# A hybrid streaming encoder on one core: diagonal blocks of the recurrent heads moved to GpSimd, one weight split moved in the pump, another lead-in

## The chip, the cores and the metric

The kernel runs on one core of a Trainium2 chip. The metric is the device time of one execution in microseconds; the number compared is the median of several runs. Engines in the profile: PE is TensorE's matmuls and PEld its weight loads, DVE is VectorE, ACT is ScalarE, POOL is GpSimd, SP is SyncE, which only issues transfers.

## The reference

One step of a one-layer encoder. A prompt of 512 new frames (no history) and a sample of 32 frames (with running state) go through the same layer: a normalisation, one wide input projection, then two branches side by side, merged by sigmoid gates, an output projection and a gated embedding. The first branch is an mLSTM with 4 heads, the second an HGRN2 with 8 recurrent heads of width 128. The change touches the second branch (and the first microseconds of the program). For one head and one chunk the reference does:

```python
g = jnp.cumsum(lf, axis=2)
dec = jnp.exp(jnp.where(causal, g[:, :, :, None, :] - g[:, :, None, :, :], -jnp.inf))
a = jnp.einsum('bhtc,bhtsc,bhsc->bhts', q, dec, k)
o = jnp.einsum('bhtc,bhce->bhte', q * jnp.exp(g), S) + jnp.einsum('bhts,bhse->bhte', a, v)
S_new = jnp.exp(g_last[:, :, 0, :])[..., None] * S + jnp.einsum('bhsc,bhse->bhce', k * jnp.exp(g_last - g), v)
```

So each query frame sees each earlier key frame through a decay of its own for every channel; a frame sees itself without decay, which is the diagonal of `a`. After that the output `o` of a head is normalised over its 128 channels and gated.

## The kernel before

**Data.** Activations lie with channels on partitions and 544 frames (32 of the sample, then 512 of the prompt) along the free axis. Each fp32 operand of a large matmul is split into a rounded high part and a low rest (`split_piece`: ScalarE casts the high part, VectorE subtracts), and a product is three matmuls: high x high, high x low, low x high, each 272 columns wide.

**Weights and the pump.** The wide projections run in pairs of output units (class `Two`) by a seven-product scheme for 2 x 2 blocks: the blocks are called a11, a12, s1, s2, s3, a22, s4, and the weight tiles carry these names and the unit's number (ws275 is s2 of unit 75). Each block is 12 matmuls in two halves of 6. The `Pump` holds all blocks of a stage in one order. One step of it is half a block: `pump.done` counts steps, and before block number i begins, `prepare(i + 1 + AHEAD)` issues the raw loads and the splits of blocks up to three ahead. `pump.behind` and `pump.pairs`, when they are set, bind a split's instructions behind another instruction of the same engine.

**Recurrent heads.** `heads()` is a generator that runs the attention of the 8 heads between the pump's steps: whatever it yields is the number of half blocks that TensorE does before it comes back, with the list `GAPS` giving most of them. TensorE's order is thus written by hand; VectorE, ScalarE and GpSimd are put in order by the compiler's scheduler, by the order of the program text and by readiness. In the profile the head's instructions lie from 628 to 876 us, with the blocks of the projections of the next heads between them, about 29.3 us a head.

Decays are applied by doubling distances: for each of 7 levels (distance 1, 2, 4, ... 64) `copies` saves the keys and queries that the level needs, `scores` makes the level's score blocks on TensorE, and `scale` multiplies keys and queries by the decay up to the next level (VectorE, L1936). Scores are made three times a head: for level 0 with the diagonal blocks (`diagonal`: 20 small matmuls), for the levels up to 8, and for the levels up to 64. Level 0 of the next head is made together with the last scores of this one. `collect` puts the scores of the levels together (VectorE's predicated copies at L1956, ScalarE's copies at L1958 and L1962). `masked` then spreads the near blocks with four GpSimd copies (L1977) and takes four triangles of 128 x 128 with GpSimd (`triangle`, L1792) into the tile `aa`.

After the last `scale(6)`, two steps later, `columns` transposes the scaled keys on TensorE (ht, L1819), `state` makes the new state (su), and some steps later `output` multiplies `aa` with the values (ho, L2012), adds the part from the state, and evacuates PSUM. The squares of the output's rows are summed on ScalarE (L2022), VectorE makes the inverse roots (L182 to L187) and scales the output (L2026), and `finish` transposes it back (hoT, L2103) and gates it (L2107).

The diagonal itself takes a path of its own in the kernel before: `collect` multiplies the diagonal blocks with a mask that keeps only their diagonals (`same`), sums each row to one number a frame (`dg`, L1953), `shares` multiplies the values with it on ScalarE (L1834, L1835) into the output tile `ov`, and `output` adds the matmuls' result on VectorE (L2018, L2019).

**Lead-in.** The first loads all go through SyncE's queue: input piece 0, first weight piece 0, input piece 1, and so on. TensorE runs 8 matmuls on a cleared tile before its first product.

Of the kernel before, what the change touches and what calls it, by code (L numbers as in the profile page):

```python
# [37 lines left out]
SUB = 5  # L38
LASTS = (0, 3, 6)
GAPS = (2, 2, 1, 3, 6, 2, 4, 2, 2, 4, 2, 8)  # L40
SLOT = 550
# [28 lines left out]
def hybrid_step(ctx: ExitStack, tc: tile.TileContext, a, o):  # L70
# [29 lines left out]
    def half(b):  # L100
        return slice(b * TH, (b + 1) * TH)
# [19 lines left out]

    def raw_piece(src, name):
        raw = wp.tile([P, WP], F32, tag="wr", name=name, bufs=NRAW)
        nc.sync.dma_start(raw[:, : src.shape[-1]], src)
        return raw
# [77 lines left out]
    def load(k):  # L203
        t = eslot(f"x{k}")
        nc.sync.dma_start(t[:, : T + 1], a["xT"][k])
        xt.append(t)
        wf.append([raw_piece(a["w_first"][k], f"wf{k}r")])

# [495 lines left out]
    class Pump:  # L704


        def __init__(self, todo):
            self.done, self.when, self.behind, self.pairs, self.limit, self.todo = 0, {}, None, None, None, todo
            order, base = [], 0
            for n, e in enumerate(todo):  # L710
# [682 lines left out]
    with tc.manual_schedule(engines={mybir.EngineType.Activation, mybir.EngineType.DVE, mybir.EngineType.PE}):  # L1393

        warm = small("warm", [P, P], bufs=1, tag="vsm")
        V.memset(warm, 0.0)
        wps = paux("warm")
# [7 lines left out]
        def products(k):  # L1405
            for f in range(NF):
                steps(acc[f], wf[k][1:], (k,), f * P, 0)

        for k in range(KD):
            t = xt[k]  # L1410
            hi, lo = pair_tile(f"x0{k}", k // (KD // 2))
            g = t[:, T : T + 1]
            S.mul(hi, t[:, :T], g)
            V.scalar_tensor_tensor(lo, t[:, :T], g, hi.bitcast(F32), ALU.mult, ALU.subtract)
            x0.append((hi, lo))
            wf[k].append(split_piece(wf[k][0], f"wf{k}", NF * P))
            if k == 1:
                load(KD - 2)
                load(KD - 1)
            sqk = slot(f"r0q{k}")[:, :T]  # L1420
            S.activation(sqk, t[:, :T], AF.Square)
            sq.append(sqk)
            if k in (1, 3):
                V.tensor_tensor(sq[k - 1], sq[k - 1], sqk, ALU.add)
            if k in (5, 6):
                i, j = ((0, 2), (4, 5))[k - 5]
                V.tensor_tensor(sq[i], sq[i], sq[j], ALU.add)
            if k > 1:
                products(k - 2)
# [368 lines left out]
    class Head:  # L1798


        def __init__(self, h):
# [7 lines left out]
            self.more = tp.tile([P, NA + 4 * NS], F32, tag="ksm", name=f"kx{h}", bufs=1)  # L1809
            self.dg, self.osb = small("dg", [P, 5]), small("osb", [P, P])  # L1810
            self.told, self.base, self.tsmp = self.tf[:, :T], 0, None
# [13 lines left out]
        def values(self):  # L1825
# [4 lines left out]
            nc.sync.dma_start(self.s0, a["S0"][self.h])  # L1830

        def shares(self):
            for b in range(NB):
                S.mul(self.ov[:, b * P : (b + 1) * P], self.it[:, b * P : (b + 1) * P], self.dg[:, b : b + 1])  # L1834
            S.mul(self.osb, self.its, self.dg[:, 4:5])  # L1835

# [86 lines left out]
        def scale(self, li):  # L1923
# [6 lines left out]
            for t, lo, m, first, _ in sides:  # L1930
# [4 lines left out]
                )  # L1935
                V.tensor_tensor(x, x, d, ALU.mult)  # L1936
            if told.shape[-1] == 2 * (nb + na):
# [6 lines left out]
            if c == NS // 2:  # L1944
                self.tsmp = tn[:, nb - 1 : nb]
            self.told = tn

        def collect(self):
            at = self.at
            if self.found[0][1] == 0:  # L1950
                same = self.kq[:, : (NB + 1) * NS].rearrange("p (b t) -> p b t", t=NS)
                V.tensor_tensor(same, self.pdg.rearrange("p (b t) -> p b t", t=NS), eye, ALU.mult)
                V.tensor_reduce(self.dg, same, AX.X, ALU.add)  # L1953
            for ps, li, c in self.found:
# [12 lines left out]
        def masked(self):  # L1967
# [39 lines left out]
        def output(self):  # L2007
# [9 lines left out]
            with tc.high_priority():  # L2017
                V.tensor_tensor(ov[:, :NP], po[:, 0, :], ov[:, :NP], ALU.add)  # L2018
                V.tensor_tensor(osb, po[:, 1, :P], osb, ALU.add)  # L2019
            hv, hr = small("hv", [P, 5]), small("hr", [P, 5])  # L2020
# [14 lines left out]
    def heads():  # L2035
# [9 lines left out]
        for h in range(HH):  # L2045
# [10 lines left out]
            x.copies(3)  # L2056
            x.shares()
            yield GAPS[3]
# [25 lines left out]
            x.collect()  # L2084
# [334 lines left out]
```

## Time and profile before

| | us |
|---|---|
| median of three runs | 1090.64 (1089.84 to 1091.63) |
| profiled execution, its own time | 1091.98 |
| its span in the trace | 1090.0 |
| TensorE matmuls busy | 1080.7 |
| VectorE busy | 897.3 |
| ScalarE busy | 700.3 |
| GpSimd busy | 217.2 |

The ends of matmuls are modelled, so a busy TensorE in this table still hides waits of a few tenths of a microsecond; they show in the starts of the matmuls. A timeline row has the start and the length in us, engine, line, operation, output and inputs, shapes and count; in brackets stands the idle time before it and what ended it. A row of a group has busy us and mean ns of one, then idle time of the engine before it.

### The profile page before, as it was taken

The page shows a single profiled execution, that of the slowest core. Times are in us where ns is not written, and L with a number is a line of the kernel's source. Part 1 is how long each engine was busy: PE and PEld are TensorE (multiplying, and loading weights), DVE is VectorE, ACT ScalarE, POOL GpSimd, SP SyncE. Part 2 cuts the span into 40 slices and gives each one's busy share as a digit, 9 for nine tenths or more (in the row PEclk, how much of TensorE's full clock was granted, in tenths as well). Part 3 has the DMA queues.
Part 4 walks back from the last instruction along what each step waited for, and adds up shares of the span by engine and source line. Part 5 has one row for each costly group of instructions (what it writes and reads, how often), then busy time and mean ns, then how long its engine had stood idle before and what let it go on. Part 6 is the DMA issues. An engine that isn't in the chain of part 4 may idle for free.

```text
span 1090.0 us, 26205 instructions
## 1 busy us (share of the span) xinstructions
PE 1080.7 (99%) x9865; PEld 1054.9 (97%) x9865; DVE 897.3 (82%) x2052; ACT 700.3 (64%) x1619; POOL 217.2 (20%) x399
## 2 busy tenths in 40 slices
PE   9999999999999999999999999999999999999998
PEld 9899999999999999999999999999999999999997
DVE  6889988676897695986888689999999887778886
ACT  7767557754666564765556488778777667446673
POOL 5205010213021122202130033223332210000002
PEclk9999999999999999999999999999999999999999
DMA  6134525648454377555599666667666783327753
GB/s 233 58 117 136 182 66 168 156 136 207 137 170 151 125 169 171 170 171 176 178 257 246 192 147 153 153 145 156 151 155 145 184 224 98 115 89 242 237 195 122
DMA packets 97270, 176.67 MB, mean 162 GB/s; under 512 B 11412, under 2 KB 18580, under 8 KB 96888
## 3 DMA queue, kind: packets, MB, share of 16 engines
q1 hardware_dynamic: 81072, 140.96, 40.1%
q0 software_dynamic: 15184, 32.93, 16.5%
q8 instruction: 77, 1.26, 0.5%
q10 hardware_dynamic: 888, 1.12, 0.3%
q14 instruction: 49, 0.40, 0.1%
HBM read 150.05 MB, written 41.69 MB: 176 GB/s over the span
## 4 chain that ended last, share of the span: by engine, by line
PE 79%; DVE 10%; ACT 6%; DMA 3%; issue 2%; SPq 0%; ACTq 0%; DVEq 0%
PE d L610 33%; PE ya L169 9%; PE yb L169 4%; PE q L169 4%; PE k L169 4%; PE C L1079 4%; PE sc L1039 2%; PE u L293 2%; PE d L462 2%; PE vp L1572 2%; PE nm L1260 2%; DVE hkq L1936 1%; PE ple L169 1%; DMA ws<-in_w_in 1%; DMA kv_d<-vhl 1%
## 5 line engine op out<-in xcount | busy, mean ns | idle before, releaser
L497 POOL DMA_DIRECT2D ws<-in_w_in x46 | 40.3, 883 | 208.8 <-DVE hkq L1936 79.8
L624 ACT COPY t<-d 128x272 f32<-128x272 f32 x153 | 57.9, 378 | 13.6 <-PE d L610 13.4
L1936 DVE TENSOR_TENSOR hkq<-hkq,q 128x288 f32<-128x288 f32 (+1 forms) x96 | 41.8, 437 | 4.4 <-ACT km L1858 3.6
L787 DVE SCALAR_TENSOR_TENSOR cv<-ub,vec,cv 128x547 f32<-128x547 f32 x48 | 37.6, 784 | 1.7 <-ACT cv L782 1.2
L1193 DVE SCALAR_TENSOR_TENSOR c<-c,wi,Cs 128x258 f32<-128x258 f32 x32 | 15.3, 479 | 18.8 <-PE Cs L1191 18.6
L1357 DVE TENSOR_TENSOR y<-ya,y 128x272 f32<-128x272 f32 x48 | 18.9, 435 | 14.3 <-PE ya L169 12.5
L1091 ACT COPY Co<-C 128x258 f32<-128x258 f32 x30 | 9.8, 378 | 27.1 <-PE C L1079 24.8
L779 POOL COPY uo<-ub 128x3 f32<-128x3 f32 x16 | 18.7, 1167 | 34.5 <-DVE ub L633 26.6
L963 POOL COPY ksm<-kf 128x96 f32<-128x96 f32 x16 | 8.1, 510 | 84.8 <-ACT kf L977 84.8
L135 POOL TENSOR_TENSOR wple50l<-wple5r,wple50h 128x256 fp32r<-128x256 f32 x1 | 0.7, 737 | 120.1 <-ACT wple50h L134 120.1
L1271 ACT COPY y<-nm 128x516 f32<-128x516 f32 x16 | 9.5, 591 | 23.0 <-PE nm L1260 22.5
L963 POOL COPY vsm<-vt 128x96 f32<-128x96 f32 x12 | 6.3, 526 | 85.9 <-ACT vt L635 43.5
L1248 DVE BATCH_NORM_STATS2 bs<-y 128x6 f32<-128x512 f32 (+1 forms) x20 | 13.8, 691 | 8.1 <-ACT y L1271 7.8
L583 POOL DMA_DIRECT2D ws<-in_w_in x14 | 14.3, 1023 | 29.8 <-DVE ws272l L135 26.6
L1260 PE MATMUL nm<-vhl,sh 128*128 128x258 f32 x112 | 18.4, 286 | 0.0
L378 POOL DMA_DIRECT2D w_pg_d<-in_w_pg x16 | 13.1, 820 | 25.3 <-issue 22.1
L1977 POOL COPY at<-at 32x128 f32<-32x128 f32 x32 | 17.9, 558 | 1.4 <-ACT at L1958 0.4
L2022 ACT ACTIVATE kit<-kq 128x128 f32<-128x128 f32 x32 | 9.7, 304 | 12.0 <-DVE kq L2018 12.0
L1008 DVE TENSOR_TENSOR ql<-q,qh 128x272 fp32r<-128x272 f32 x24 | 9.4, 434 | 8.3 <-ACT qh L1007 7.2
L378 POOL DMA_DIRECT2D w_out_d<-in_w_out x16 | 13.5, 1005 | 12.7 <-issue 10.6
L1260 PEld LDWEIGHTS nm<-vhl,sh 128*128 128x128 f32 x112 | 15.5, 190 | 0.6 <-ACT Co L1091 0.5
L1792 POOL TENSOR_SCALAR_AFFINE_SELECT aa<-at 128x128 f32<-128x128 f32 x32 | 15.7, 523 | 0.6
(4748 smaller groups left out, 5112.5 us busy)
## 6 DMA issues: line engine op xcount, KB each, us to landing
ws<-in_w_in POOLq DMA_DIRECT2D x60, 256.0 KB, 5.1
ws<-in_w_in SPq DMA_DIRECT2D x46, 256.0 KB, 4.0
ya_d<-y SPq DMA_DIRECT2D x32, 272.0 KB, 2.3
y<-ya_d SPq DMA_DIRECT2D x24, 272.0 KB, 3.6
w_out_d<-in_w_out POOLq DMA_DIRECT2D x24, 256.0 KB, 6.2
w_pg_d<-in_w_pg POOLq DMA_DIRECT2D x24, 256.0 KB, 6.3
c<-in_C SPq DMA_DIRECT2D x16, 258.0 KB, 3.6
out_Cs<-c SPq DMA_DIRECT2D x16, 258.0 KB, 3.7
```

The costliest lines, as they stand in the source:

```text
L169: PE.matmul(both[b][:m, :TH], part(w, off + k * step, m, x), xx[:, half(b)], start=(k == 0 and j == 0), stop=(k == n - 1 and j == 2),)
L293: PE.matmul(both[b][:m, :TH], part(w, off + k * step, m, x), xx[:, half(b)], start=(k == 0 and j == 0), stop=(k == KD - 1 and j == 2),)
L378: G.dma_start(late[g][n][k], src, accum_op=ALU.add)
L462: PE.matmul(self.ps[b][:, : c.stop - c.start], part(self.w, k * P, P, x), xx[:, c], start=(k == 0 and j == 0), stop=(k == KD - 1 and j == 2),)
L497: G.dma_start(t, piece(u, i), accum_op=ALU.add)
L610: PE.matmul(ps, ww[:, c], xx, start=(start and k == 0 and j == 0), stop=end, skip_group_check=not start,)
L624: self.kept = S.copy(t, ps)
L787: V.scalar_tensor_tensor(cv[:, :547], ub[:, j : j + 547], vcol(V_CW + 4 * ft + j), cv[:, :547], ALU.mult, ALU.add)
L1039: PE.matmul(pn[:, 0, :n], ks[f][x][:, j * P : (j + 1) * P], qs[f][y][:, NS + j * P : T], start=(f == 0 and i == 0), stop=(f == KH - 1 and ...
L1079: PE.matmul(pn[g][:, :VH], kw[b][x][:, f * P : (f + 1) * P], vv[b][y][:, g * VH : (g + 1) * VH], start=(b == 0 and j == 0), stop=(b == NB ...
L1260: PE.matmul(pn[:, g, :VH], st[j][x][:, (i - j) * P : (i - j + 1) * P], vv[j][y][:, g * VH : (g + 1) * VH], start=(j == 0 and q == 0), stop ...
L1936: V.tensor_tensor(x, x, d, ALU.mult)
```

## The change

- The masked diagonal blocks (`same`) are no longer summed to `dg`. `masked` adds them with GpSimd onto the triangles in `aa`: one addition for each group of 32 partitions (4 x 32 numbers each), and one of 32 x 32 for the sample. `shares`, the tile `dg` and the row sum go. `output` evacuates PSUM with two ScalarE copies. The order of the diagonal blocks' columns changes to match `aa`.
- In `heads`, for the last two steps ahead of the last scores of a head (`LAG = 2`) the pump prepares one block less ahead; after `scale(6)` its look-ahead is restored, `prepare` is called again with `pump.pairs` set to the last multiplication of the scaling, and `pump.pairs` is cleared.
- The warm-up matmuls read the built-in zero constant. The first two first-weight pieces are loaded through ScalarE's queue. For piece 0 VectorE rounds the weights, the input is split in two halves, and the products go term by term: high x high for all outputs, then the low input, then the low weights.

```diff
-    def raw_piece(src, name):
+    def raw_piece(src, name, queue=None):
...
-        wf.append([raw_piece(a["w_first"][k], f"wf{k}r")])
+        wf.append([raw_piece(a["w_first"][k], f"wf{k}r", nc.scalar if k < 2 else nc.sync)])
...
-                self.prepare(i + 1 + AHEAD)
+                self.prepare(i + 1 + self.ahead)
...
-        warm = small("warm", [P, P], bufs=1, tag="vsm")
-        V.memset(warm, 0.0)
+        warm = nc.const_aps.tensor(0.0, [P, P], F32)
...
+                first = [wp.tile([P, WP], F32R, tag=tag, name=f"wf0{tag}") for tag in ("wh", "wl")]
+                wh, wl = (x[:, : NF * P] for x in first)
+                V.tensor_copy(wh, wf[0][0][:, : NF * P])
+                for b in range(2):
+                    S.mul(hi[:, half(b)], t[:, half(b)], g)
+                    V.scalar_tensor_tensor(
+                        lo[:, half(b)], t[:, half(b)], g, hi[:, half(b)].bitcast(F32), ALU.mult, ALU.subtract
+                    )
+                V.tensor_tensor(wl, wf[0][0][:, : NF * P], wh.bitcast(F32), ALU.subtract)
...
-        def shares(self):
-            for b in range(NB):
-                S.mul(self.ov[:, b * P : (b + 1) * P], self.it[:, b * P : (b + 1) * P], self.dg[:, b : b + 1])
-            S.mul(self.osb, self.its, self.dg[:, 4:5])
...
-            for b, (c, _, _) in enumerate(chunks + ((csmp, 0, 0),)):
+            for c, i, j in chunks + ((csmp, 0, 2),):
+                b = 2 * j + i
...
-                V.tensor_reduce(self.dg, same, AX.X, ALU.add)
...
+            for g in range(QUADS):
+                k = slice(g * NS, (g + 1) * NS)
+                d = self.aa[k].rearrange("p j b t -> p (j b) t")[:, :, k]
+                G.tensor_tensor(d, d, self.same[k, :NB], ALU.add)
+            G.tensor_tensor(self.near[:NS, 2 * NS :], self.near[:NS, 2 * NS :], self.same[:NS, NB], ALU.add)
...
-                V.tensor_tensor(ov[:, :NP], po[:, 0, :], ov[:, :NP], ALU.add)
-                V.tensor_tensor(osb, po[:, 1, :P], osb, ALU.add)
+                S.copy(ov[:, :NP], po[:, 0, :])
+                S.copy(osb, po[:, 1, :P])
...
-            x.shares()
...
-                yield GAPS[6]
+                yield GAPS[6] - LAG
+                pump.ahead = AHEAD - 1
+                yield LAG
             else:
-                yield GAPS[11]
+                yield GAPS[11] - LAG
+                pump.ahead = AHEAD - 1
+                yield LAG
...
-            x.scale(6)
+            pump.pairs = x.scale(6)
+            pump.ahead = AHEAD
+            pump.prepare(pump.done // 2 + AHEAD)
+            pump.pairs = None
```

More of the change, by code (lines that the diff above doesn't have):

```diff
@@ L39 @@
 LASTS = (0, 3, 6)
+LAG = 2
 GAPS = (2, 2, 1, 3, 6, 2, 4, 2, 2, 4, 2, 8)
@@ L120, in psplit @@
         return hi, lo
-    def raw_piece(src, name):
+    def raw_piece(src, name, queue=None):
         raw = wp.tile([P, WP], F32, tag="wr", name=name, bufs=NRAW)
-        nc.sync.dma_start(raw[:, : src.shape[-1]], src)
+        (queue or nc.sync).dma_start(raw[:, : src.shape[-1]], src)
         return raw
@@ L708, in __init__ @@
             self.done, self.when, self.behind, self.pairs, self.limit, self.todo = 0, {}, None, None, None, todo
+            self.ahead = AHEAD
             order, base = [], 0
@@ L1405, in products @@
         def products(k):
-            for f in range(NF):
-                steps(acc[f], wf[k][1:], (k,), f * P, 0)
+            if k:
+                for f in range(NF):
+                    steps(acc[f], wf[k][1:], (k,), f * P, 0)
+                return
+            for j, (x, xx) in enumerate(((0, x0[0][0]), (0, x0[0][1]), (1, x0[0][0]))):
+                for f in range(NF):
+                    for b in range(2):
+                        PE.matmul(
+                            acc[f][b][:, :TH],
+                            part(wf[0][1:], f * P, P, x),
+                            xx[:, half(b)],
+                            start=(j == 0),
+                            stop=False,
+                        )
         for k in range(KD):
@@ L1412, in hybrid_step @@
             g = t[:, T : T + 1]
-            S.mul(hi, t[:, :T], g)
-            V.scalar_tensor_tensor(lo, t[:, :T], g, hi.bitcast(F32), ALU.mult, ALU.subtract)
             x0.append((hi, lo))
-            wf[k].append(split_piece(wf[k][0], f"wf{k}", NF * P))
+            if k:
+                S.mul(hi, t[:, :T], g)
+                V.scalar_tensor_tensor(lo, t[:, :T], g, hi.bitcast(F32), ALU.mult, ALU.subtract)
+                wf[k].append(split_piece(wf[k][0], f"wf{k}", NF * P))
+            else:
+                first = [wp.tile([P, WP], F32R, tag=tag, name=f"wf0{tag}") for tag in ("wh", "wl")]
+                wh, wl = (x[:, : NF * P] for x in first)
+                V.tensor_copy(wh, wf[0][0][:, : NF * P])
+                for b in range(2):
+                    S.mul(hi[:, half(b)], t[:, half(b)], g)
+                    V.scalar_tensor_tensor(
+                        lo[:, half(b)], t[:, half(b)], g, hi[:, half(b)].bitcast(F32), ALU.mult, ALU.subtract
+                    )
+                V.tensor_tensor(wl, wf[0][0][:, : NF * P], wh.bitcast(F32), ALU.subtract)
+                wf[0].append(first)
             if k == 1:
@@ L1809, in __init__ @@
             self.more = tp.tile([P, NA + 4 * NS], F32, tag="ksm", name=f"kx{h}", bufs=1)
-            self.dg, self.osb = small("dg", [P, 5]), small("osb", [P, P])
+            self.osb = small("osb", [P, P])
             self.told, self.base, self.tsmp = self.tf[:, :T], 0, None
@@ L1935, in scale @@
                 )
-                V.tensor_tensor(x, x, d, ALU.mult)
+                last = V.tensor_tensor(x, x, d, ALU.mult)
             if told.shape[-1] == 2 * (nb + na):
@@ L1946, in scale @@
             self.told = tn
+            return last
         def collect(self):
@@ L1950, in collect @@
             if self.found[0][1] == 0:
[L1951 to L1953 removed]
+                self.same = self.kq[:, : (NB + 1) * NS].rearrange("p (b t) -> p b t", t=NS)
+                V.tensor_tensor(self.same, self.pdg.rearrange("p (b t) -> p b t", t=NS), eye, ALU.mult)
             for ps, li, c in self.found:
```

## The prediction

> **What bounds the kernel now.** I read the page's busy shares first, then the busy time of one head's stretch, then the waits of the recurrent stretch (607 to 870 us, where all that the diff touches lies but the lead-in), then the timelines of each engine around those waits.
>
> ```profile
> PE 1080.7 (99%) x9865; PEld 1054.9 (97%) x9865; DVE 897.3 (82%) x2052; ACT 700.3 (64%) x1619; POOL 217.2 (20%) x399
> ```
>
> ```profile
> 678.00:707.00 29.00, 28.79 (x403) 27.70 (x401) 26.59 (x78) 22.55 (x66) 9.12 (x17) 1.00 0.68 154
> ```
>
> TensorE is the bound throughout: its matmuls follow one another in an order written by hand, so a microsecond on another engine counts only where TensorE waits for it. In one head's 29 us VectorE is busy 26.59 us (third sum), ScalarE 22.55, GpSimd 9.12. VectorE is nearly full and late in places:
>
> ```profile
> PEld ht L1819 <- DVE hkq L1936: 2.5, 10, 0.3
> PE hoT L2103 <- DVE kq L2026: 0.5, 3, 0.2
> PEld pl L1885 <- ACT kx L1858: 0.4, 1, 0.4
> PEld d L610 <- DVE ws276l L135: 0.4, 1, 0.4
> ...
> PEld d L610 <- DVE ws274l L135: 0.3, 1, 0.3
> ```
>
> Columns: who waited for whom, us in total, times, longest; of the four late split weights the first and the last are shown (0.4, 0.4, 0.4, 0.3). These are real gaps: the four key transposes behind the last scaling take 0.94 us, the same four of the values 0.60 (third head).
>
> ```profile
> 706.50 0.94 PE L1819 MATMUL ht<-ident,hkq 128*128 128x128 f32 x4
> ...
> 717.29 0.60 PE L1819 MATMUL ht<-ident,hi 128*128 128x128 f32 x4
> ```
>
> The recoverable time is thus 2.5 (key transposes) + 0.5 (output transposes) + 1.5 (four late split weights) + 0.4 (one late copy) = 4.9 us of 1090.
>
> **The change, part by part.** *Splits behind the last scaling.* VectorE in the third head:
>
> ```profile
> 704.21 0.69 DVE L135 TENSOR_TENSOR wa1152l<-wi52r,wa1152h 128x512 fp32r<-128x512 f32 x1
> 704.82 0.69 DVE L135 TENSOR_TENSOR wa1252l<-wi52r,wa1252h 128x512 fp32r<-128x512 f32 x1
> 705.42 0.69 DVE L135 TENSOR_TENSOR wa2275l<-wi67r,wa2275h 128x512 fp32r<-128x512 f32 x1
> 706.02 0.42 DVE L1936 TENSOR_TENSOR hkq<-hkq,q 128x256 f32<-128x256 f32 x1
> ```
>
> Three weight splits stand ahead of the scaling, 0.60 us apart. The pump looks one block less ahead for two steps, so the third split (wa2275l) falls behind it: scaling and score collection start 0.60 sooner, and the 0.34 of waiting (0.94 - 0.60) goes. I take the whole 2.5. The split's own matmuls come two blocks after the transposes, past 12 matmuls and the state sums, so a split 2 us later is hidden; were that cover gone, it would cost its 0.69 once a head, 5.5 us. The block's raw loads move with it by at most a block.
>
> *Shares and sum.* Per head go, from VectorE, a reduction and two adds out of PSUM, the larger 0.687; from ScalarE five multiplications; ScalarE gets two copies out of PSUM, the larger like the transposes' 0.588.
>
> ```profile
> L1834 ACT ACTIVATE kq<-hi,dg 128x128 f32<-128x128 f32 x32 | 12.4, 389 | 0.0
> L2018 DVE TENSOR_TENSOR kq<-ho,kq 128x512 f32<-128x512 f32 x8 | 5.5, 687 | 0.8 <-PE ho L2016 0.8
> L1822 ACT COPY hkq<-ht 128x512 f32<-128x512 f32 x8 | 4.7, 588 | 0.8 <-ACT at L1962 0.6
> ```
>
> ScalarE's five at 0.389 (1.9 us) stood between the squares whose sums start the output's normalisation, so that chain ends over 1 us sooner and frees VectorE of a backlog. I credit all of the output transposes (0.5), the late copy, which queued behind these multiplications (0.4), and the four split weights (1.5; the third head's waited behind the output scaling):
>
> ```profile
> 698.33 0.74 DVE L2107 SCALAR_TENSOR_TENSOR ob<-hoT,vec,hg 128x512 f32<-128x512 f32 x1
> 698.99 0.68 DVE L135 TENSOR_TENSOR ws275l<-ws,ws275h 128x512 fp32r<-128x512 f32 x1
> ```
>
> The diagonal's 20 matmuls a head only change places: nothing.
>
> *GpSimd's adds.* Four adds of 32 partitions x 128 numbers, and a 32 x 32 one, follow the triangles; the first output matmul (ho<-hi,aa) then waits for all four. No such add is in the trace. Nearest rows, mean ns:
>
> ```profile
> L1024 POOL TENSOR_TENSOR qw<-qf,wi 128x32 f32<-128x32 f32 x16 | 5.9, 375 | 21.8 <-ACT qf L1004 21.7
> L2287 POOL TENSOR_TENSOR h<-h,rows 128x272 f32<-128x272 f32 x6 | 4.5, 777 | 55.2 <-ACT rows L2283 55.2
> L135 POOL TENSOR_TENSOR wple60l<-wple6r,wple60h 128x256 fp32r<-128x256 f32 x1 | 0.9, 935 | 0.0
> ```
>
> The ends are 0.375 and 0.935, since its 128 numbers lie between 32 and 256; on the line through the first two, 128 numbers take 0.375 + 0.402 x 96/240 = 0.536. I take that, since size sets it. The time left for them is what lies between the last triangle and the first output matmul (heads 0, 2, 4, 5, 7):
>
> ```profile
> 649.15 4.62 POOL L1977 COPY at<-at 32x128 f32<-32x128 f32 x4 [0.44 <-ACT at L1958]
> 653.84 1.58 POOL L1792 TENSOR_SCALAR_AFFINE_SELECT aa<-at 128x128 f32<-128x128 f32 x4
> ...
> 707.16 1.85 POOL L1977 COPY at<-at 32x128 f32<-32x128 f32 x4
> 709.09 2.21 POOL L1792 TENSOR_SCALAR_AFFINE_SELECT aa<-at 128x128 f32<-128x128 f32 x4
> 713.38 0.88 POOL L497 DMA_DIRECT2D ws<-in_w_in  x1 [2.08 <-DVE ws252l L135]
> ...
> 767.78 2.21 POOL L1792 TENSOR_SCALAR_AFFINE_SELECT aa<-at 128x128 f32<-128x128 f32 x4
> ...
> 798.15 2.02 POOL L1792 TENSOR_SCALAR_AFFINE_SELECT aa<-at 128x128 f32<-128x128 f32 x4
> ...
> 859.33 1.03 POOL L1792 TENSOR_SCALAR_AFFINE_SELECT aa<-at 128x128 f32<-128x128 f32 x4
> ```
>
> ```profile
> 655.26 0.61 PE L2012 MATMUL ho<-hi,aa 128*128 128x128 f32 x4
> ...
> 713.79 0.60 PE L2012 MATMUL ho<-hi,aa 128*128 128x128 f32 x4
> ...
> 772.23 0.60 PE L2012 MATMUL ho<-hi,aa 128*128 128x128 f32 x4
> ...
> 801.72 0.49 PE L2012 MATMUL ho<-hi,aa 128*128 128x128 f32 x3
> ...
> 861.24 0.61 PE L2012 MATMUL ho<-hi,aa 128*128 128x128 f32 x4
> ```
>
> Slack: head 0 -0.16, head 2 2.49 (1 and 3 alike), head 4 2.24 (6 alike), head 5 1.55, head 7 0.88. Collection starts 0.60 sooner and TensorE arrives 0.34 sooner: 0.26 more each, so 0.10, 2.75, 2.50, 1.81, 1.14. The adds need 4 x 0.536 + 0.08 (the handover 709.01 to 709.09) = 2.22. Left over: head 0 2.12, head 5 0.41, head 7 1.08, the others none. In head 0 the copies took 4.62 against 1.85; at 1.85 its stall is gone. I take the middle, 1.06. The stalls add up to 2.6 us. At 0.375 the need is 1.58 and they are 0.7 (half of head 0's 1.48) + 0.4 = 1.1; the other end is priced as a rival. The small add runs while the first output matmuls do. GpSimd's transfers behind the adds (713.38) start at most a microsecond later; they are for a unit several blocks away, so no cost; without that cover it is that microsecond, once a head.
>
> The Trainium skill (GPSIMD Engine Reference, section 3.1) gives some 2.6 cycles for each element of a two-input operation at 1.2 GHz, 2.17 ns; the two rows give 0.402/240 = 1.68 ns. By the page an add is estimated at 0.375 + 96 x 2.17 ns = 0.58 us, and the stalls grow from 2.6 to about 3.3.
>
> *Lead-in.* Warm-up reads a constant instead of a tile that VectorE clears; two weight loads go to ScalarE's queue; the first piece is rounded on VectorE, its input in halves.
>
> ```profile
> 0.80 0.39 SPq L205 DMA_DIRECT2D x<-in_xT  x1
> 1.12 3.78 PE L1399 MATMUL warm<-warm 128*128 128x128 f32 x16 [1.12 <-DVE emc L1242]
> 3.53 0.75 ACT L1413 ACTIVATE x<-x 128x544 fp32r<-128x544 f32 x1 [1.44 <-DMA x<-in_xT]
> 4.73 1.28 PE L293 MATMUL u<-x,wf0h 128*128 128x272 f32 x4
> ```
>
> Warm-up waited for VectorE's clearing (1.12) and can start when other engines do, 0.80, or 0.32 sooner, and so the products at 4.41; half an input takes about 0.40, so 3.53 + 0.40 = 3.93 is in time, even with the load 0.45 later for sharing the engines. The early matmuls run slowly (4 in 1.28); if that stretch ends when it did, only about half is kept. Between 0.16 and 0.32 I take 0.25. SyncE's later loads move up by two issues; ScalarE's two issues end before 3.53.
>
> Sum: 4.9 + 0.25 - 2.6 = 2.6 us gained. The profiled execution took 1091.98, so 1089.4; it was 1.34 above the median of the three runs, 1090.64, so 1088.0 there.
>
> **Rivals.** *Slower: GpSimd ends last in every head.* Four triangles took 2.21 us beside VectorE's splits but 1.03 in head 7: GpSimd slows beside VectorE. The wple60l row ran so. At 0.935 an add, 3.82 are needed: stalls 3.7 + 3 x 1.1 + 2 x 1.3 + 2.0 + 2.7 = 14.3, time 1099.8; at 0.80 it is 1095. Counting head 0 in full, gain and stalls balance at 0.64 an add, and 0.72 costs 0.2%. Against it: the size. The Trainium skill (GPSIMD Engine Reference, section 1) says that GpSimd shares its SBUF interfaces with VectorE and contends with instructions that have two SBUF inputs, which the splits have; the triangles agree.
>
> *The split doesn't move.* The third head's scores lie between these two:
>
> ```profile
> 703.20 0.29 PE L610 MATMUL d<-xfh,ws375l 128*128 128x272 f32 x1
> ...
> 704.78 0.39 PE L610 MATMUL d<-xfh,ws375h 128*128 128x272 f32 x1
> ```
>
> That is the middle of the block of ws375, so the step count is odd, and the catch-up call behind the scaling asks for no more than is prepared; the held block is prepared at the next block's start, unbound. Only its later place in the text then puts it behind. If VectorE's order stays, the 2.5 stays and GpSimd starts no sooner: stalls 1.2 + 0.7 + 1.3 = 3.2 against 2.65 gained, 1091.2, within the noise. For it: the scaling must be ready when the split would be; its scores are done when the products resume at 704.78, before 705.42, which speaks against.
>
> *Better.* Head 0's copies at 1.85 and GpSimd beside a lighter VectorE: no stalls, 1090.64 - 4.9 - 0.25 = 1085.5. Against it: nothing in the trace of before says why those copies were slow.
>
> **Chances.** Forecast 0.45 (its own range 1086.6 to 1089.6), slower rival 0.20, no move 0.20, better 0.15. A measurement tells 0.2%, 2.2 us, from no change. Faster: 0.37 of the forecast and all of the better case, 0.52; same: 0.08 + 0.18 + 0.04 = 0.30; slower: 0.18. The range leaves out most of the slower rival: 1085.2 to 1092.0.
>
> **What would show it.** The key transposes at about 0.60 in all heads, the third split behind the scaling; no waits of output transposes or s2 weights on VectorE; adds near 0.54 and waits of ho on GpSimd in heads 0, 5 and 7 alone; warm-up at 0.80. Adds over 0.64, or ho waiting in the middle heads, make it wrong.

## The result, and the profile after

The changed kernel takes 1106.97 us, the median of four runs (1103.40 to 1110.52), against 1090.66 for the kernel before: a ratio of 1.0148, with a 95% interval of 1.0131 to 1.0164. The forecast was 1088.0, with a range of 1085.2 to 1092.0. One execution of run 2 below took 2473.2 us; it is left out of that run's median and ratio. The profiled execution took 1108.18 us; its span is 1106.5.

The page of the changed kernel, busy shares first, as read before:

```profile
PE 1082.3 (98%) x9865; PEld 1057.3 (96%) x9865; DVE 894.0 (81%) x2029; ACT 700.4 (63%) x1595; POOL 242.2 (22%) x439
```

TensorE is busy 1.6 us longer than before and the span is 16.5 us longer, so TensorE stands still for most of the difference. Who it waited for (us in total, times, longest):

```profile
PE ho L2038 <- POOL aa L2006: 13.1, 8, 2.6
PE hoT L2135 <- DVE kq L2052: 2.3, 1, 2.3
...
PEld ht L1844 <- DVE hkq L1957: 0.4, 1, 0.4
```

The first row is new: the score-weighted output waits for GpSimd's additions in all eight heads. The last row, of the weight loads, answers to the 2.5 us of the key transposes in the prediction, which are nearly gone. The third head shows it, four transposes in 0.60 us where they took 0.94:

```profile
712.31 0.60 PE L1844 MATMUL ht<-ident,hkq 128*128 128x128 f32 x4
```

GpSimd in one middle head, the sixth, 807 to 817 us (start, length, then what the idle time before ended with):

```profile
807.40 0.92 POOL L2007 TENSOR_TENSOR at<-at,kq 32x32 f32<-32x32 f32 x1 [1.24 <-DVE at L1977]
808.28 2.34 POOL L1998 COPY at<-at 32x128 f32<-32x128 f32 x4
810.69 1.86 POOL L1817 TENSOR_SCALAR_AFFINE_SELECT aa<-at 128x128 f32<-128x128 f32 x4
812.63 0.88 POOL L498 DMA_DIRECT2D ws<-in_w_in  x1
813.24 2.85 POOL L2006 TENSOR_TENSOR aa<-aa,kq 32x128 f32<-32x128 f32 x4
816.04 0.87 POOL L584 DMA_DIRECT2D ws<-in_w_in  x1
```

Three things differ from the forecast here. The small 32 x 32 addition runs first, ahead of the copies, and not beside the output's matmuls. The issue of a transfer stands between the triangles and the additions (0.6 us from 812.63 to 813.24). It stands there in the second to the seventh head, and in the third and fourth it waits there itself for another transfer to land, 0.70 and 1.12 us, with the additions behind it:

```profile
718.28 0.88 POOL L498 DMA_DIRECT2D ws<-in_w_in  x1 [0.70 <-DMA ws<-in_w_in]
...
751.07 0.89 POOL L498 DMA_DIRECT2D ws<-in_w_in  x1 [1.12 <-DMA ws<-in_w_in]
```

And the additions take 0.71 us each, as the group row says:

```profile
L2006 POOL TENSOR_TENSOR aa<-aa,kq 32x128 f32<-32x128 f32 x32 | 22.7, 710 | 1.6
```

And VectorE in the third head, around the last scaling:

```profile
709.26 0.68 DVE L136 TENSOR_TENSOR wa1252l<-wi52r,wa1252h 128x512 fp32r<-128x512 f32 x1
709.86 0.68 DVE L136 TENSOR_TENSOR wa2275l<-wi67r,wa2275h 128x512 fp32r<-128x512 f32 x1
710.46 0.68 DVE L136 TENSOR_TENSOR ws475l<-ws,ws475h 128x512 fp32r<-128x512 f32 x1
711.06 0.42 DVE L1957 TENSOR_TENSOR hkq<-hkq,q 128x256 f32<-128x256 f32 x1
...
712.09 0.26 DVE L1977 COPY_PREDICATED at<-lmask,pl 128x96 f32<-128x96 uint8 x1
```

The third split (wa2275l) was to move behind the scaling; it stands ahead of it still, and a fourth (ws475l) with it. The predicated copy that starts the collection ran one row behind the scaling's first multiplication before (706.02, 706.36); it now runs three behind.

The wait of 2.3 us ahead of the output transposes stands in the first head alone, and it came by way of a transfer. GpSimd issues it behind the additions, 1.0 us later than before (656.96; 655.97 in the kernel before), and it lands after 7.9 us, where it took 6.1. ScalarE's cast waits for it, the split ws450l on VectorE waits for the cast, and the inverse roots of the first head's output stand behind that split on VectorE. In the kernel before, the same cast found its tile there (last row).

```profile
656.96 1.17 POOL L584 DMA_DIRECT2D ws<-in_w_in  x1
...
664.96 0.62 ACT L135 CAST ws450h<-ws 128x512 fp32r<-128x512 f32 x1 [2.03 <-DMA ws<-in_w_in]
...
665.61 0.69 DVE L136 TENSOR_TENSOR ws450l<-ws,ws450h 128x512 fp32r<-128x512 f32 x1 [1.98 <-ACT ws450h L135]
...
663.55 0.60 ACT L134 CAST ws450h<-ws 128x512 fp32r<-128x512 f32 x1
```

Two of the waits did more than their own length. Below are two stretches right behind the two longest waits (2.3 us ahead of the output transposes of the first head, 2.6 us ahead of the output of the third), then the stretch of a whole head, which holds a wait of 1.6 us; the columns are the busy times of TensorE's matmuls and weight loads, VectorE, ScalarE and GpSimd, then granted clock, DMA share and GB/s.

```profile
671.50:675.00 3.50, 3.45 (x17) 3.48 (x18) 2.54 (x6) 3.32 (x8) 0.86 (x1) 0.53 0.82 156
722.00:725.50 3.50, 3.38 (x19) 3.38 (x20) 0.87 (x4) 0.00 (x0) 1.95 (x4) 0.63 0.99 222
680.37:710.53 30.16, 28.60 (x412) 28.00 (x404) 25.98 (x76) 23.15 (x64) 12.35 (x21) 1.00 0.65 147
```

The clock fell to 0.53 and 0.63 there; in the kernel before, no stretch of the heads is below 1.00. The third head's output shows the wait, and the low clock behind it:

```profile
722.12 0.71 PE L2038 MATMUL ho<-hi,aa 128*128 128x128 f32 x4 [2.57 <-POOL aa L2006]
...
723.72 0.63 PE L2038 MATMUL ho<-hi,aa 128*128 128x128 f32 x2
```

The first four took 0.60 before. The 0.1 more is not the clock: they take 0.71 in the other heads too, behind waits that left the clock at 1.00. The pair at 723.72 took 0.39 before. The Trainium skill (TensorE: Matmul & The Clock Gate, Part 1) tells of a gate that halves the clock after a window of about 3.4 us without work. The halving agrees; here 2.3 and 2.6 us of standing were enough, and the waits of 1.0 to 1.7 us in the other heads were not. Length alone does not decide: a wait of 2.31 us in run 2 (third head's output) and one of 2.26 in run 11 (output transposes at 705.51) left the clock at 1.00.

The account, from the starts of TensorE's matmuls in the heads (628 to 876 us), after against before, summed over the heads: ahead of the output +14.4; the output's own matmuls +2.0 (1.2 of it the third head at the low clock); ahead of the output transposes +1.3 (2.4 in the first head, less 0.3 to 0.4 gained in each of three others); ahead of the state sums and in them +1.1; transposes of keys and values -2.0; the rest -0.5. Sum +16.3, and the last matmul starts 16.2 later. The rest hides two larger terms: products at the low clock cost 1.7, and the four late split weights gained 1.6. With the output's 1.2 the low clock cost some 3 us.

### The profile page after: what moved, and what is told of

Read it like the earlier page. It is cut to its first block, busy times and chain, and to the rows that moved or that the text cites. A ratio compares the mean times of both kernels' runs of the same rounds, so it can differ in the third digit from the quotient of the medians.

```text
span 1106.5 us, 26244 instructions
## 1 busy us (share of the span) xinstructions
PE 1082.3 (98%) x9865; PEld 1057.3 (96%) x9865; DVE 894.0 (81%) x2029; ACT 700.4 (63%) x1595; POOL 242.2 (22%) x439
## 3 DMA queue, kind: packets, MB, share of 16 engines
q0 software_dynamic: 15184, 32.93, 16.3%
## 4 chain that ended last, share of the span: by engine, by line
PE 77%; DVE 6%; POOL 5%; ACT 4%; DMA 4%; issue 3%; SPq 0%; DVEq 0%; ACTq 0%; POOLq 0%
PE d L611 32%; PE ya L170 9%; PE yb L170 4%; PE q L170 4%; PE k L170 4%; PE C L1081 4%; PE nm L1262 3%; PE sc L1041 2%; DMA ws<-in_w_in 2%; PE d L463 2%; PE vp L1597 2%; PE u L294 2%; POOL aa L2006 2%; POOL at L1998 1%; DVE hkq L1957 1%
## 5 line engine op out<-in xcount | busy, mean ns | idle before, releaser
L1359 DVE TENSOR_TENSOR y<-ya,y 128x272 f32<-128x272 f32 x48 | 18.8, 434 | 14.3 <-PE ya L170 12.5
L2038 PE MATMUL ho<-hi,aa 128*128 128x128 f32 x64 | 12.3, 296 | 13.1 <-POOL aa L2006 13.1
L2038 PEld LDWEIGHTS ho<-hi,aa 128*128 128x128 f32 x64 | 9.4, 197 | 14.8 <-POOL aa L2006 14.8
L2006 POOL TENSOR_TENSOR aa<-aa,kq 32x128 f32<-32x128 f32 x32 | 22.7, 710 | 1.6
L2319 POOL TENSOR_TENSOR h<-h,rows 128x272 f32<-128x272 f32 x6 | 4.5, 776 | 54.6 <-ACT rows L2315 54.6
L1998 POOL COPY at<-at 32x128 f32<-32x128 f32 x32 | 16.2, 506 | 1.0
```

The costliest lines, as they stand in the source:

```text
L1998: G.tensor_copy(at[k, :NA].rearrange("p (b q s t) -> p b q s t", b=2, q=2, s=2)[:, :, g // 2], both_)
L2006: G.tensor_tensor(d, d, self.same[k, :NB], ALU.add)
```

## Experiments

Rows of waits in this section are TensorE's, of the run under which they stand.

**1. No additions.** From the changed kernel:

```diff
-                G.tensor_tensor(d, d, self.same[k, :NB], ALU.add)
...
-            G.tensor_tensor(self.near[:NS, 2 * NS :], self.near[:NS, 2 * NS :], self.same[:NS, NB], ALU.add)
```

> The changed kernel without its five GpSimd additions in each recurrent head; it leaves the heads' masked diagonal blocks out of the result, and keeps the new binding of the splits, ScalarE's plain copies and the lead-in. Theory A (GpSimd ends last: five additions of 0.71 and 0.92 us stand between the masks and the score-weighted output's matmuls, which waited 13.1 us in all for them): that wait nearly goes, the two stretches of half clock go with it, and the time is 1086 to 1089 us, the prediction's gain of 4 us or less. Rival B (the later binding of the splits, with its hoT wait of 2.3 us and the colder clock, costs the time): 1100 us or more. Rival C (ScalarE's copies in place of the VectorE additions, or the lead-in): 1095 us or more.

1092.28 us; against before 1.0005 (0.9996 to 1.0014). The wait for GpSimd is gone and with it the loss and the low clock, so theory A holds for the 16 us. But the gain is not there either: 1086 to 1089 was expected. The waits that the changed kernel had lost are back:

```profile
PE ht L1844 <- DVE hkq L1957: 1.7, 6, 0.4
...
PE su L2009 <- ACT hkq L1847: 0.8, 4, 0.2
PE hoT L2130 <- DVE kq L2047: 0.6, 1, 0.6
```

In the changed kernel TensorE had stood still for 13 us elsewhere; I take it that VectorE caught up in that time.

**2. The diagonal's path alone**, on the kernel before (additions in; sums, shares and VectorE's additions out):

```diff
-                V.tensor_reduce(self.dg, same, AX.X, ALU.add)
...
+                G.tensor_tensor(d, d, self.same[k, :NB], ALU.add)
...
-                V.tensor_tensor(ov[:, :NP], po[:, 0, :], ov[:, :NP], ALU.add)
+                S.copy(ov[:, :NP], po[:, 0, :])
...
-            x.shares()
```

> The kernel before with the diagonal blocks' path alone changed (GpSimd additions in, the diagonal sums, ScalarE's shares and the VectorE additions out); splits bound as before, lead-in as before. Theory A: the additions' waits come back (13 to 15 us on the output's matmuls) and the key transposes' wait of 2.5 us stays: 1102 to 1112 us. If the copies' start sets the end as well, the earlier key scaling of the kernel before does not help it. Rival B (the binding of the splits costs the time): 1090 to 1094 us. Rival C (lead-in): the same as B.

1114.07 us, the median of three executions (1109.81 to 1116.77), 1.0203 (1.0172 to 1.0234). That is at the upper end of theory A's range or just above it. In the profile (of the execution of 1109.81 us), two heads are worse than in the changed kernel, the first and the fourth, by 3.1 and 1.7 us ahead of the output; in the second, third, fifth, sixth and seventh the stalls are within 0.3 us of its own. I had expected the key transposes' wait to stay; it went here too, without the new binding. So the binding was not needed for it, and in the changed kernel the third split had not moved.

```profile
PE ho L2012 <- POOL aa L1980: 17.2, 8, 4.1
```

GpSimd in the first head, where four copies take 4.85 us:

```profile
649.71 4.85 POOL L1972 COPY at<-at 32x128 f32<-32x128 f32 x4
```

**3. Binding and lead-in without the diagonal's change**, and **5. the binding alone**, on the kernel before:

```diff
-                yield GAPS[6]
+                yield GAPS[6] - LAG
+                pump.ahead = AHEAD - 1
+                yield LAG
...
-            x.scale(6)
+            pump.pairs = x.scale(6)
+            pump.ahead = AHEAD
+            pump.prepare(pump.done // 2 + AHEAD)
+            pump.pairs = None
```

> The changed kernel with the diagonal blocks' path of the kernel before put back; the new binding of the splits and the new lead-in stay. Theory A: the key transposes' wait (2.5 us) and the output transposes' (0.5 us) are recovered and nothing of GpSimd's is added: 1086 to 1089 us. Rival B: 1098 us or more, with waits of the output transposes for split weights. Rival C for the lead-in: 1093 us or more.

> The kernel before with only the new binding of the splits (one block less ahead for two steps, and the catch-up behind the last scaling). My prediction's step (the binding frees the key transposes of their 2.5 us): 1088 to 1089 us and no key transposes behind the scaling left waiting. Rival, after the run that had the binding and the lead-in without the diagonal's change (1093.4 us, with the key transposes at 0.46 us but the next head's value transposes 0.3 to 0.4 us longer from head 2 on): the wait only moves, 1091 to 1094 us.

1093.4 us, 1.0020 (1.0011 to 1.0030), and 1092.92 us, 1.0019 (1.0010 to 1.0028): slightly slower, both. With VectorE's old load the binding does move the third split behind the scaling, and no key transpose waits. The wait moves to the first product behind the next head's value transposes and to the output transposes, here of run 5:

```profile
PE d L611 <- DVE hkq L632: 1.0, 4, 0.3
PE hoT L2113 <- DVE kq L2029: 0.8, 4, 0.3
```

In run 5, over the heads, the key transposes gain about as much (2.4 us) as the value transposes lose; the state sums and the output transposes, with the products ahead of them, lose 1.9 more.

**4. The additions on VectorE**, all five, in the changed kernel:

```diff
-                G.tensor_tensor(d, d, self.same[k, :NB], ALU.add)
+                V.tensor_tensor(d, d, self.same[k, :NB], ALU.add)
```

> The changed kernel with the same five additions issued on VectorE in place of GpSimd; nothing is left out. Theory A (the place of the additions is what costs): VectorE takes each in some 0.15 to 0.35 us behind the masks, so the output's matmuls wait 0 to 0.8 us in a head, 0 to 6 us in all, in place of 13.1: 1087 to 1096 us. A variant of A in which the masks themselves are late (they ended 6.3 to 7.2 us after the scores in both kernels) gives the lower end. Rival B or C: 1103 us or more, as the changed kernel. If VectorE's queue, in order, holds its additions until GpSimd's masks are there and so holds its own splits, the waits move to the dense matmuls behind them and the time is 1095 to 1105 us.

1105.03 us, 1.0124 (1.0109 to 1.0139): at the edge of the case named last, but the waits moved mostly to another place. VectorE adds in 0.283 us, and stands 12.4 us for GpSimd's triangles ahead of it. The output transposes wait 9.0 us instead, products 3.4. The triangles, with VectorE standing beside them, take 0.287 us each, where they took 0.533 in the changed kernel (last row):

```profile
L2006 DVE TENSOR_TENSOR aa<-aa,kq 32x128 f32<-32x128 f32 x32 | 9.1, 283 | 12.7 <-POOL aa L1817 12.4
L1817 POOL TENSOR_SCALAR_AFFINE_SELECT aa<-at 128x128 f32<-128x128 f32 x32 | 8.2, 287 | 0.6
...
L1817 POOL TENSOR_SCALAR_AFFINE_SELECT aa<-at 128x128 f32<-128x128 f32 x32 | 16.0, 533 | 0.6
```

**6. The lead-in alone** on the kernel before: the constant for the warm-up, the two loads on ScalarE's queue, and piece 0 in halves, as in the change's diff.

> The kernel before with only the new lead-in. My prediction: 0.25 us faster, within 0.2% in any case. Rival: the first input now lands later (4.2 to 4.5 us against 3.5 in the profiles), the warm-up ends before it and TensorE stands 0.3 to 0.6 us, so that the early matmuls run at the low clock for longer: 0.5 to 2 us slower and a wider spread of the runs.

1091.19 us, 0.9996 (0.9987 to 1.0005): no difference that can be measured. In the runs' profiles the products of the second weight piece start 0.8 us sooner to 1.3 us later than before with this lead-in, and 0.1 to 0.7 sooner with the old one (a run compared with another run), so a single profile says little of it.

**7. VectorE's and ScalarE's relief alone**: run 2 without the additions.

```diff
-                G.tensor_tensor(d, d, self.same[k, :NB], ALU.add)
...
-            G.tensor_tensor(self.near[:NS, 2 * NS :], self.near[:NS, 2 * NS :], self.same[:NS, NB], ALU.add)
```

> The kernel before without the diagonal's sums, shares and VectorE additions, with ScalarE's plain copies, and without GpSimd's additions (the heads' masked diagonal blocks are left out of the result); splits and lead-in as before. Theory (taking the reduction and the two additions off VectorE, and the five multiplications off ScalarE, is what freed the key transposes, the output transposes and the s2 weights; the binding adds nothing): all of the 4.9 us come, 1084.5 to 1087 us. Rival (the relief needs the binding, or only the additions' stalls gave VectorE the time to catch up): 1089.5 to 1092.5 us, as the changed kernel without its additions (1092.3).

1091.42 us, 1.0001 (0.9993 to 1.0010): the rival. The account shows a wash. Over the heads the scores and the products ahead of them (behind the output transposes) gain 2.2 us, the output transposes and the products ahead of them 0.5, the transposes of keys and values 0.2; the products ahead of these lose 0.8, and the state sums with the products ahead of them 2.2. VectorE in the third head says why (of this run):

```profile
703.12 0.68 DVE L135 TENSOR_TENSOR wa2275l<-wi67r,wa2275h 128x512 fp32r<-128x512 f32 x1
705.33 0.69 DVE L135 TENSOR_TENSOR ws475l<-ws,ws475h 128x512 fp32r<-128x512 f32 x1 [1.52 <-ACT ws475h L134]
705.94 0.42 DVE L1932 TENSOR_TENSOR hkq<-hkq,q 128x256 f32<-128x256 f32 x1
```

And ScalarE:

```profile
704.68 0.62 ACT L134 CAST ws475h<-ws 128x512 fp32r<-128x512 f32 x1 [1.95 <-DMA ws<-in_w_in]
```

With less on VectorE the scheduler puts one more split, ws475l, ahead of the last scaling (in the kernel before it stands behind it). Its raw tile comes by a transfer that has not landed: ScalarE waits for the transfer, VectorE for ScalarE, and the scaling behind them, whose scores were done at about 703.9, starts at 705.94. The changed kernel has the same order; there, behind its stalls, the transfer had landed and nothing waited for it at this place.

**8. The small addition last.**

```diff
-                G.tensor_tensor(d, d, self.same[k, :NB], ALU.add)
-            G.tensor_tensor(self.near[:NS, 2 * NS :], self.near[:NS, 2 * NS :], self.same[:NS, NB], ALU.add)
+                end = G.tensor_tensor(d, d, self.same[k, :NB], ALU.add)
+            with tc.issue_after(end.ins):
+                G.tensor_tensor(self.near[:NS, 2 * NS :], self.near[:NS, 2 * NS :], self.same[:NS, NB], ALU.add)
```

> The changed kernel with the sample's 32 x 32 addition bound behind the last of the four others. In the changed kernel's trace it ran first, 0.9 us ahead of the copies. Theory A: GpSimd's copies, masks and additions are one queue that ends last, so the output's matmuls wait 0.7 to 0.9 us less a head: 1099 to 1102 us. Rival (the copies wait for VectorE's or ScalarE's last collecting copy, which comes after the small addition's end in any case, so its place costs nothing): 1104 to 1108 us.

1108.03 us, 1.0153 (1.0139 to 1.0167): theory A's form of it fails. The copies start up to 0.7 us sooner and the triangles and additions take as much longer; in the fifth head, whose scores stand within 0.03 us of the changed kernel's, the additions end at 785.52 us, there at 785.53:

```profile
779.40 2.31 POOL L1817 TENSOR_SCALAR_AFFINE_SELECT aa<-at 128x128 f32<-128x128 f32 x4
781.66 0.90 POOL L498 DMA_DIRECT2D ws<-in_w_in  x1
782.25 3.27 POOL L2006 TENSOR_TENSOR aa<-aa,kq 32x128 f32<-32x128 f32 x4
```

**9. The output two half blocks later** in the changed kernel.

```diff
-            yield GAPS[1]
+            yield GAPS[1] + (GAPS[10] if last else 0)
             if last:
                 last.output()
-                yield GAPS[10]
...
-        yield GAPS[9]
+        yield GAPS[9] + 2
```

> The changed kernel with the score-weighted output two half blocks (some 1.6 us) later in TensorE's order. Theory A (GpSimd's end against the output's place is what costs): the middle heads' stalls of 1.8 us shrink to 0.2 to 0.4, those of heads 2 and 3 by 1.6, the stretches of half clock go: 13 us of stalls become about 3, and since the run without additions stood at 1092.3 us, the time is 1093 to 1096 us. Rival (GpSimd is late because it waits for TensorE or VectorE work that moves along): 1103 us or more.

1105.40 us, 1.0136 (1.0111 to 1.0161). No output matmul waits for GpSimd any more, and the time is that of the changed kernel all the same:

```profile
PE hoT L2134 <- DVE kq L2052: 10.8, 7, 3.2
```

What follows the output (copies, squares, inverse roots, scaling) takes as long as before and the output transposes have a fixed place: the wait moved there. My expectation counted only the first of two places.

**10. The binding kept two steps longer, no additions**, so that wa2 and ws4 stand behind the scaling:

```diff
-            pump.pairs = None
             x.collect()
             x.masked()
...
             yield GAPS[7]
+            pump.pairs = None
```

> The changed kernel without its additions (the heads' masked diagonal blocks are left out of the result), and with the binding behind the last scaling kept for two more steps, so that the splits wa2 and ws4 stand behind it on VectorE; without that, ws4's split stood ahead of the scaling and waited there for its transfer through ScalarE's cast (1.3 to 1.5 us idle in the profiles). Theory D (the 4.9 us of waits did not come back because the freed VectorE was given ws4's split ahead of the scaling, where it waits): the key transposes' and state sums' waits go, 1086.5 to 1089.5 us against 1092.3. Rival (as with the binding alone, what is held back is late next, at the next head's query transposes, or the normalisation bounds the stretch): 1091 to 1094 us.

1090.67 us, 0.9993 (0.9982 to 1.0004). Half of theory D: the key transposes and state sums no longer wait (key transposes -2.4 us over the heads), and the output transposes wait in their place:

```profile
PE hoT L2130 <- DVE kq L2047: 4.4, 6, 1.3
```

**11. The edits of runs 9 and 10 together, with the additions.**

> The whole change, nothing left out, with both: the output two half blocks later and the binding kept for two more steps. Theories A and D: 1087 to 1092 us, the kernel before or a little faster. If D fails and A holds: 1092 to 1096 us. If both fail: above 1100 us.

1111.68 us, 1.0188 (1.0170 to 1.0207): the case that both theories fail, with 15.5 us of waits at the output transposes.

**12 to 14. The output transposes two half blocks later too**, in the kernels of run 10 (12), of run 11 (13) and before (14):

```diff
             yield GAPS[4]
-            if last:
-                finish(h - 1)
             x.scale(4)
             x.copies(5)
             yield GAPS[5]
+            if last:
+                finish(h - 1)
```

> The run with the binding kept two steps longer and no additions (the heads' masked diagonal blocks are left out of the result), with the output transposes and the gating of the head before two half blocks later. Theory E (the forecast waits are real, and each cure shifted them to the next place fixed by hand in TensorE's order; there, in the run before, the output transposes waited 4.4 us): with that place moved too, the waits of the heads go, 1086 to 1088.5 us. Rival F (VectorE and ScalarE set the pace of a head, so that waits turn up elsewhere): 1089.5 to 1093 us with new waits of 3 us or more.

> The whole change, nothing left out, with all three moves: output two half blocks later, binding kept two steps longer, output transposes two half blocks later. Theory A and E: the output's and the output transposes' waits (15.5 us in the run with two of the moves) shrink to 4 us or less, 1088 to 1094 us. Rival F: waits of 8 us or more remain at the output transposes or turn up at the value transposes, 1098 us or more.

> The kernel before with only the output transposes and the gating two half blocks later: a control for the two runs sent with it. Its output transposes waited 0.5 us and its late s2 splits 1.5. Theory E: at most these 0.5 to 1 us come, 1089.5 to 1091.5 us, so that a gain in the other two is not this move's own. Rival: 1087 to 1089 us, the move alone is the gain; or, if the gating's later end holds up the scores' scaling behind it, 1092 to 1095 us.

Run 12: 1089.38 us, 0.9979 (0.9970 to 0.9988). Run 14, the control: 1091.78 us, 1.0000 (0.9991 to 1.0009). So with both places moved some 2.3 us of the 4.9 do come, if nobody has to add the diagonal. The time lies between the two theories' ranges: E is right in kind and F in part, since 1.9 us turn up at products of s3 (ws374 and others), which wait for ScalarE to evacuate PSUM:

```profile
PE d L611 <- ACT t L625: 1.9, 4, 0.7
```

Run 13: 1101.09 us, 1.0081 (1.0067 to 1.0095), F: 7.3 us at the output transposes and 5.4 at the products stay.

**15. Four such additions where VectorE has nothing to do**, at the start of the kernel before; one execution, for the rows.

```diff
+    dum = tp.tile([P, 2, 2, P], F32, tag="kws", name="dum", bufs=1)
+    G.memset(dum, 0.0)
+    for g in range(4):
+        k = slice(g * 32, (g + 1) * 32)
+        d = dum[k].rearrange("p j b t -> p (j b) t")[:, :, k]
+        G.tensor_tensor(d, d, ident[k].rearrange("p (b t) -> p b t", t=32), ALU.add)
```

> The kernel before with four more GpSimd additions of the same shape (32 partitions x 4 x 32 numbers, in place) at the program's start, where VectorE has nothing to do from 1.1 to 4.3 us. It is run for the duration of these four rows. In the changed kernel's heads such an addition took 0.44 to 1.31 us, 0.71 in the mean. Theory G (the additions are slow because VectorE's two-input instructions run beside them): 0.40 to 0.48 each here, below my estimate of 0.536. Rival (0.71 is what such an addition costs): 0.65 or more each.

```profile
2.03 1.96 POOL L221 TENSOR_TENSOR dum<-dum,ident 32x128 f32<-32x128 f32 x4
...
4.58 0.55 POOL L321 COPY cmask<-cmask 32x32 f32<-32x32 f32 x1
...
5.63 0.20 POOL L321 COPY cmask<-cmask 32x32 f32<-32x32 f32 x1
```

VectorE in the same stretch has nothing between these rows:

```profile
1.06 0.06 DVE L1248 MEMSET emc<- 128x1 f32 x1
4.25 0.81 DVE L1420 SCALAR_TENSOR_TENSOR x<-x,x 128x544 fp32r<-128x544 f32 x1 [3.14 <-ACT x L1419]
4.99 0.56 DVE L135 TENSOR_TENSOR wf0l<-wf0r,wf0h 128x384 fp32r<-128x384 f32 x1
```

Four additions in 1.96 us, 0.49 each: just over theory G's range, and far from the rival's 0.65. My 0.536 was thus near the undisturbed price; beside VectorE it is 0.71. The same copy of 32 x 32 took 0.55 us while VectorE ran a two-input operation (4.25 to 5.06) and 0.20 after. The Trainium skill (GPSIMD Engine Reference, section 1) names this sharing of SBUF interfaces, and these rows agree.

**16. The old path of the diagonal with the rest**: run 3's kernel with the edits of runs 10 and 12; nothing is left out.

> The changed kernel with the diagonal's path of the kernel before (nothing is left out and GpSimd adds nothing), the binding kept two steps longer and the output transposes two half blocks later. Theory E with VectorE's old load: the key transposes' 2.5 us go, the output transposes no longer wait, and of the value transposes' new wait (0.4 us a head with the binding alone) part stays: 1088 to 1090.5 us, 0.1 to 0.3% under the kernel before. Rival F (VectorE paces the head): 1090.5 to 1093 us.

1090.97 us, 0.9992 (0.9983 to 1.0002): between the two, and no difference that can be measured. No run with the whole computation beat the kernel before.

## Why the prediction was wrong

**The step that failed: GpSimd's additions.** I had 2.6 us of stalls, in three heads; they were 14.4, in all eight. Three terms of the sum were off. The addition: 0.536 taken, 0.710 measured, because I let size decide (run 15: 0.49 alone) and gave a busy VectorE no weight in the sum, although the triangles' 0.55 against 0.26 in the last head stood in the prediction, with the rival that rests on them. The queue: the small addition was to run beside the output's matmuls, and it runs ahead of the copies; a transfer's issue stands ahead of the additions (0.6 us), where I had put the transfers behind them, and in two heads it waits there (0.70 and 1.12). Run 8 shows, however, that taking the small addition out from ahead buys nothing: GpSimd's rows behind it stretch by as much. That the rest of the queue and VectorE's work beside it fix the end is my reading. The slack: 0.26 us more a head was to come from an earlier collection. In the middle heads it did not, since the splits stayed ahead of the scaling and the predicated copy fell back: in five of heads 1 to 6 the triangles end 1.8 to 1.9 us ahead of where the output would have followed the matmul before it; 1.81 to 2.75 were forecast.

The rows give the size of each term. From the last triangle's end to the last addition's end, the eight heads take 29.7 us, where 8 x 2.22 = 17.8 were forecast. Of the 11.9 us between, 7.0 are the additions themselves (24.1 us with their handovers, 17.2 forecast) and 4.9 what stands between triangles and additions, the transfers' issues and their waits. The slack adds up to 15.7, against 16.3: what most middle heads lack, the first, the fourth and the last have more. In the first, the copies took 1.95 us here, as the better case had it.

A fourth term was put at nothing: GpSimd's transfers behind the additions, "at most a microsecond" later and at no cost. One of them, issued 1.0 us later and 1.8 us longer under way (why, no run shows), is behind the 2.3 us ahead of the first head's output transposes and the low clock that followed.

The rival with GpSimd ending last in every head had the place right, 14.3 us of stalls, and put it at 1099.8 with a chance of 0.20. Its mechanism was an addition at 0.935; nearly the same sum came about at 0.71 with the issues ahead, so that the agreement of 14.3 with 14.4 is luck. By the prediction's own working, 0.71 an addition would give some 7 us of stalls. (That working also gives 3.0, not about 3.3, at 0.58 an addition.) What the rival did not have is what a stall does to the clock, some 3 us.

**The gain of 4.9 us.** The waits named were read rightly, but "recoverable" was wrong, and this is the second error. In the changed kernel, the key transposes gained nearly what was forecast, and the output transposes behind the first head did; without the additions the key transposes did not (runs 1 and 7), so I put their gain down to TensorE's standing elsewhere. The four late split weights gained 1.6 us in runs 1 and 7 too, and the state sums lost 2.1 and 2.2 there. The late copy (0.4) did not gain: TensorE waits for it 0.3 us (its weight load 0.4 to 0.5) in every run, also where the multiplications are gone. Without the additions the whole rest is worth nothing (1.0005), the relief alone nothing (1.0001), the binding alone -0.2%. Each wait removed came back at the next place that TensorE's hand-written order fixes: key transposes to value transposes (run 5), output transposes to key transposes and state sums (run 7), these to the output transposes (run 10). With two places moved, 2.3 us were measured (run 12). I priced the split that is held back at nothing because its own matmuls come two blocks later; it is not its matmuls that wait but what VectorE does behind it.

**The split doesn't move.** This rival (0.20) was right of the changed kernel and wrong of the binding: alone, it does move the split (run 5). Beside the diagonal's change it does nothing visible in the middle heads, because the scheduler has meanwhile moved two splits ahead of the scaling (run 7), where the binding does not reach them; kept two steps longer it does (run 10).

**What was right**: the lead-in within 0.2% (run 6), the gain at the late split weights, and the signs by which the prediction was to be known as wrong (the output waiting in the middle heads).

What stays open: how much of the 14.4 us would go if one of the terms alone went, since run 8 shows that they stretch each other; and why the first head's four copies took 4.6 us before and 4.85 in run 2, but 1.95 in the changed kernel.

## What to carry to other kernels

A wait in a trace is worth its length only if what stands behind it on the waiting engine's queue is ready sooner too: look at which place in the order fixed by hand comes next, and whether the engine that was late has slack by then. Work given to an idle engine must be priced beside what its neighbour runs at that moment, and its whole queue counted to the point where somebody waits, transfers' issues included. And when an order is made by a scheduler, taking work off an engine moves other work: here a split ahead of the work that mattered, to wait for a transfer.

## What was not expected of the hardware

Standing still for 2.3 us once, and 2.6 once, was followed by 3.5 us at a granted clock of 0.53 and 0.63 in the mean, though TensorE had been at the full clock for over 600 us; two other waits of 2.3 us (runs 2 and 11) were not. And GpSimd's operations are stretched beside VectorE's: the same addition took 0.49 us alone and 0.71 in the mean beside VectorE, a triangle 0.287 with VectorE standing (run 4) and 0.533 beside it. VectorE's seem to be stretched in turn: a split beside the additions of the sixth head took 0.93 us (814.25), the next one, as they ended, 0.68 (816.05).
